# Mixer inputs taken from unscaled x and scaled out of PSUM, gate operands fetched from DRAM, LRU factor by exp, MLP operands at mixed spacing

## The chip, the cores and the metric

The kernel runs on one core of one Trainium2 chip. Its engines are TensorE (PE; its weight loads are listed as PEld), VectorE (DVE), ScalarE (ACT), GpSimd (POOL) and SyncE (SP, which issues DMAs here). The metric is device time in microseconds; lower is better.

## The reference

One decoder layer on 16 meta tokens and 512 tokens (T = 528) of width 2048, in float32:

```python
u = rmsnorm(h, norm1_g)
v_pool, v_lru, v_gelu, g_pool, g_lru = jnp.split(u @ w_in, ...)      # five times 2048
pool_out = pool_mixer(v_pool, pool_w, pool_scale)                    # window means, 512x512 maps
xc = causal_depthwise_conv(v_lru, conv_w, conv_b)                    # width 4
lru_out = rg_lru(xc, ...) * gelu(v_gelu)                             # h_t = a_t h_(t-1) + bt
merged = sigmoid(g_pool) * pool_out + sigmoid(g_lru) * lru_out
h = h + merged @ w_out
h = h + jnp.square(relu(rmsnorm(h, norm2_g) @ mlp_w1)) @ mlp_w2      # inner width 8192
out = rmsnorm(h, final_g)[:, 16:]
```

In `rg_lru`, r and i are sigmoids of 256x256 maps of each head of xc, a = exp(-8·r·softplus(-lam)) and bt = sqrt(1 - a²)·i·xc.

## The kernel before

Features lie on the 128 partitions, tokens on the free axis. Every float32 product is made of three matmuls: weights and inputs are split into a hi and a lo part (hi in the short fp32r format, lo = value - hi), and `mm3s` and `mm3` (matmul lines L332, L337) add hi·hi, hi·lo and lo·hi in PSUM. The class `Weights` runs through all weight chunks in one fixed order: SP loads a raw chunk (L94), VectorE forms sums for Strassen where wanted (L109, tile `sum`, or in place in `w21`), ACT writes `whi` (L117), VectorE `wlo` (L118). It works two chunks ahead of TensorE.

Each engine takes its instructions in the order in which the code was written, unless the framework puts one further on for priority. The stages, by time in the trace:

- Start and mixer, 0 to 515 us. A string of `jobs` sets the order: V2, VR, VL and VP are in_proj jobs (V2 and VL for the LRU branch, VR and VP for the pool branch; 96 matmuls of 264 columns for each 128 features, V2 and VR make two), GA_h holds the LRU gates of head h, PW_g the pool maps of group g, F_k forms Strassen operands of the normalised x for the later gates. V2 and VL_2 multiply x·g1 before the norm's scale is known (`split_x`), and their results are multiplied with `scale` in VR. While they run, ACT and DVE or POOL sum the squares; in VL_2 at k = 8 `norm1` adds them over the partitions and forms `scale` (a reciprocal and a Newton step). In VR every k's input is then scaled and split again (`rescale_x`, L361 to L363), and all further jobs use that. x lies in tile `a1`, as two halves of TH = 264 tokens (8 meta and 256 tokens), hi and lo blocks of 264 elements.
- `conv` makes xc and its hi and lo parts (`xs`, L454, L455), GA runs 48 matmuls and then tanh, sqrt, a reciprocal 1/(1+t) (L485), and the scan. in_proj results leave PSUM by ACT (`evac`, L408).
- Gates, 515 to 984: the three gated parts of w_in for the 512 tokens, 24 Strassens of 7 products. Each product is 24 matmuls of 256 columns and has one operand: x11, x21, x22 (quarters of x), t1 to t4 (their sums). x11, x21 and x22 are read straight from the blocks of 264 in `a1`, t2, t3 and t4 are brought from DRAM (`fill`, by POOL's queue), t1 stays in `a2`.
- w_out to 1176; first MLP matrix (w1), 1176 to 1788, 32 Strassens of the same kind with operands x11 ... t4 in blocks of 256; second MLP matrix (w2), 1788 to 2425, in 38 steps of 7 products over a window of eight slots in `a1`, `a2` and `slot0`, which hold t2, t4, t3, t1, x21, x22, x11 of one hidden block each (hi half, then lo half) and are split as they arrive; then the final norm to 2478.

A1's free space is counted in PL = 16·264 elements; HS is 256, `place(i)` names seven places for an operand.

## Time and profile before

| what | us |
|---|---|
| median of three runs | 2481.21 (2481.19 to 2487.64) |
| profiled execution | 2479.7 |
| its span in the trace | 2477.9 |
| TensorE busy | 2401.4 (97%) |
| VectorE busy | 1983.6 (80%) |
| ACT busy | 1196.9 (48%) |
| POOL busy | 288.5 (12%) |
| DMA moved | 407.71 MB, 165 GB/s mean |

The span runs from the first to the last instruction in the trace. Busy shares are means over stages that differ; what an engine does in one stage is read from that stage's window. "a" in a row is tile a1 or a2, "gs" a gate's sigmoid, "rx" rescaled x, "ga", "ps_vl", "ps_vp", "ps_vr" PSUM tiles of the jobs with those names.

### The profile page before, as it was taken

How to read it: one execution, taken by the hardware profiler on the slowest of the kernel's cores; microseconds unless marked ns; L12 is line 12 of the kernel's file. 1: busy time of each engine (PE TensorE's matmuls, PEld its weight loads, DVE VectorE, ACT ScalarE, POOL GpSimd, SP SyncE). 2: the span in 40 equal slices, each digit the busy share in tenths (PEclk: the TensorE clock that was granted, in tenths of full speed). 3: DMA queues.
4: the chain of work that ended last, by engine and by line, in shares of the span. 5: the costliest groups of instructions: out<-in, count | busy, mean ns of one | idle time of the engine just before them, and what ended most of it. 6: DMA issues, size and time to landing. Idle time of an engine off the chain costs nothing. (4 is left out here: it accounts for less than half of the span.)

```text
span 2477.9 us, 46247 instructions
## 1 busy us (share of the span) xinstructions
PE 2401.4 (97%) x19286; PEld 2345.5 (95%) x19286; DVE 1983.6 (80%) x2371; ACT 1196.9 (48%) x1639; POOL 288.5 (12%) x377
## 2 busy tenths in 40 slices
PE   7899999999999999999899999999989999999997
PEld 7899999989999999887899999999989999999996
DVE  8867676678888887368898889888788888888778
ACT  6444434345555555244444444444455555555445
POOL 2123232220000001022000000000100000000010
PEclk9999999999999999999999999999989999999999
DMA  5244443354444446567545444544565666665553
GB/s 208 77 141 137 158 136 137 127 187 139 147 143 145 139 143 246 193 203 256 192 159 168 155 156 161 168 153 156 211 174 158 189 179 184 181 179 174 150 167 106
DMA packets 114065, 407.71 MB, mean 165 GB/s; under 512 B 13440, under 2 KB 20736, under 8 KB 112448
## 3 DMA queue, kind: packets, MB, share of 16 engines
q1 hardware_dynamic: 78224, 251.82, 31.5%
q0 software_dynamic: 35488, 152.85, 19.1%
q8 instruction: 150, 2.46, 0.4%
q14 instruction: 59, 0.48, 0.1%
q10 hardware_dynamic: 144, 0.10, 0.0%
HBM read 319.91 MB, written 84.80 MB: 163 GB/s over the span
## 5 line engine op out<-in xcount | busy, mean ns | idle before, releaser
L118 DVE TENSOR_TENSOR wlo<-raw,whi 128x1024 fp32r<-128x1024 f32 (+6 forms) x403 | 468.1, 1164 | 167.3 <-ACT whi L117 164.1
L117 ACT ACTIVATE whi<-raw 128x1024 fp32r<-128x1024 f32 (+6 forms) x403 | 402.8, 1002 | 412.3 <-issue 105.1
L117 ACT ACTIVATE whi<-sum 128x1024 fp32r<-128x1024 f32 (+5 forms) x282 | 282.0, 1000 | 471.4 <-DVE sum L109 226.8
L118 DVE TENSOR_TENSOR wlo<-sum,whi 128x1024 fp32r<-128x1024 f32 (+5 forms) x282 | 322.5, 1144 | 89.7 <-ACT whi L117 85.6
L337 PE MATMUL ps_A<-a,whi 128*128 128x256 f32 x2048 | 357.4, 278 | 4.0 <-ACT p L600 1.7
L337 PE MATMUL ps_Ab<-a,whi 128*128 128x256 f32 x1728 | 315.4, 282 | 1.4 <-ACT u_b L622 0.7
L337 PEld LDWEIGHTS ps_A<-a,whi 128*128 128x128 f32 x2048 | 310.9, 189 | 5.9 <-ACT p L600 1.9
L337 PE MATMUL ps_A<-a,wlo 128*128 128x256 f32 x1024 | 283.9, 277 | 0.6 <-DVE wlo L118 0.6
L337 PEld LDWEIGHTS ps_Ab<-a,whi 128*128 128x128 f32 x1728 | 265.3, 189 | 2.5 <-ACT u_b L622 1.1
L337 PE MATMUL ps_Ab<-a,wlo 128*128 128x256 f32 x864 | 243.2, 282 | 0.0
L109 DVE TENSOR_TENSOR sum<-sum,raw 128x1024 f32<-128x1024 f32 (+7 forms) x188 | 215.2, 1145 | 5.6
L337 PEld LDWEIGHTS ps_A<-a,wlo 128*128 128x128 f32 x1024 | 193.3, 189 | 0.9 <-DVE wlo L118 0.8
L337 PE MATMUL ps_B<-a,whi 128*128 128x256 f32 x1024 | 178.6, 277 | 1.9 <-DMA a<-gsp_x 1.9
L337 PEld LDWEIGHTS ps_Ab<-a,wlo 128*128 128x128 f32 x864 | 166.2, 192 | 0.1
L337 PE MATMUL ps_Bb<-a,whi 128*128 128x256 f32 x864 | 158.3, 282 | 0.0
L337 PE MATMUL ps_wo<-a,whi 128*128 128x512 f32 x512 | 158.0, 390 | 0.0
L337 PEld LDWEIGHTS ps_B<-a,whi 128*128 128x128 f32 x1024 | 154.9, 189 | 2.1 <-ACT u L622 2.1
L332 PE MATMUL ps_vp<-a,whi 128*128 128x264 f32 x896 | 146.2, 285 | 7.5 <-ACT gs L471 4.8
L332 PE MATMUL ps_vl<-a,whi 128*128 128x264 f32 x896 | 146.1, 285 | 0.7 <-ACT gs L471 0.6
L337 PE MATMUL ps_B<-a,wlo 128*128 128x256 f32 x512 | 141.9, 277 | 0.3 <-DVE wlo L118 0.3
L337 PEld LDWEIGHTS ps_Bb<-a,whi 128*128 128x128 f32 x864 | 132.8, 189 | 0.0
L332 PEld LDWEIGHTS ps_vp<-a,whi 128*128 128x128 f32 x896 | 124.3, 188 | 8.4 <-ACT gs L471 5.5
(319 smaller groups left out, 5748.3 us busy)
## 6 DMA issues: line engine op xcount, KB each, us to landing
raw<-w SPq DMA_DIRECT2D x168, 512.0 KB, 4.2
raw<-w_in SPq DMA_DIRECT2D x135, 512.0 KB, 3.5
w<-w SPq DMA_DIRECT2D x56, 512.0 KB, 4.3
a<-ysp POOLq DMA_DIRECT2D x27, 896.0 KB, 6.4
hsp<-e POOLq DMA_DIRECT2D x32, 512.0 KB, 6.8
ysp<-t POOLq DMA_DIRECT2D x31, 512.0 KB, 4.4
w<-w_in SPq DMA_DIRECT2D x24, 512.0 KB, 3.5
ysp<-y POOLq DMA_DIRECT2D x31, 384.0 KB, 5.0
```

The source lines that it names most:

```text
L109: nc.vector.tensor_tensor(self.raw[o], self.raw[x], self.raw[y], op=ALU.add)
L117: nc.scalar.activation(hi[:, s], raw[:, s], AF.Copy)
L118: nc.vector.tensor_tensor(lo[:, s], raw[:, s], hi[:, s].bitcast(F32), op=ALU.subtract)
L332: PE.matmul(o, a, r, start=first and i == 0, stop=last and i == 2)
L337: PE.matmul(o, a, b, start=first and i == 0, stop=last and i == 2, skip_group_check=True)
```

## The change

The mixer's in_proj jobs all multiply the split of unscaled x·g1. `rescale_x` is gone; `norm1` runs in VR at k = 4. V2 and VL_2 leave PSUM by ACT as before and are multiplied with `scale` later; all other jobs leave PSUM by a multiplication with `scale` on VectorE. The first step of conv goes from VectorE to ACT. In `a1` the 528 tokens of a part follow each other, parts start every 576 elements (16 more for k of 8 and over). VL_3 comes before GA_0. The `xs` tiles lie in the pool of the Strassen sums, whose `w21` chunks can be loaded only after GA_7. In GA the reciprocal is replaced by exp(-2·...) on ACT, an addition of 1, and two scalar-tensor-tensor steps on VectorE (a Newton step from that start). F writes six operands to DRAM instead of three, and the gates' x11, t2, x21, t3 and x22 are fetched after VP_15, t4 after GA_7 and PW_3. In the gates x22 alone now has blocks every 264 elements, in w1 t4 alone, where all were at 256. In w2 the slots start every 3648 elements in `a1` (3584 before), a slot holds the values (then lo) first and hi after, and x11's hi part is moved by 0, 8, ..., 40 elements in six of nine slots; a slot is split in two pieces.

```diff
+SW = 2 * T
+XW = 576
...
-        self.free = {"raw": raw_bufs, "w21": 2}
+        self.free = {"raw": raw_bufs, "w21": 0}
...
-    def place(i):
+    def place(i, width=HS):
+        if width > HS:
+            return [tuple(a1[:, i * PL + (8 * j + k) * width : i * PL + (8 * j + k) * width + HS]
+                          for j in range(2)) for k in range(8)]
...
-    def fill(i, src, n):
-        if i < 6:
+    def fill(i, src, n, width=HS):
+        if width > HS:
+            t = a1[:, i * PL : i * PL + 16 * width].rearrange("p (a k n) -> p a k n", a=2, k=8)
+            src = src.rearrange("p a (k n) -> p a k n", k=8)
+            for j in range(2):
+                G.dma_start(t[:, j, :n, :HS], src[:, j, :n].bitcast(F32R))
+        elif i < 6:
...
     def ux(k, part):
...
-        a, kk = k // 8, k % 8
-        t = a1[:, 2 * a * PL : 2 * (a + 1) * PL].rearrange("p (b n) -> p b n", b=2)
-        at = part * 8 * TH + kk * TH
-        return t[:, :, at : at + TH]
+        at = (2 * k + part) * XW + 16 * (k // 8)
+        return a1[:, at : at + T]
...
-    jobs = "V2_0 VL_2 VR_0 GA_0 VL_3 VP_2 GA_1 VP_3 VL_4 PW_0 VL_5 F_0 VP_4 GA_2 VP_5 F_1 VL_6 VP_6 F_2 VL_7"
+    jobs = "V2_0 VL_2 VR_0 VL_3 GA_0 VP_2 GA_1 VP_3 VL_4 PW_0 VL_5 F_0 VP_4 GA_2 VP_5 F_1 VL_6 VP_6 F_2 VL_7"
...
+        V.tensor_scalar(sp8, sp4, -2.0, None, op0=ALU.mult)
...
-    f_sp = {r: dram.tile([P, 2, 8 * HS], F32, name=f"fsp_{r}") for r in ("t2", "t3", "t4")}
+    f_sp = {r: dram.tile([P, 2, 8 * HS], F32, name=f"fsp_{r}") for r in ("x11", "t2", "x21", "t3", "x22", "t4")}
...
         def split_x(k):
-            S.activation(ux(k, 0), blocks(ht[:, k]), AF.Copy, scale=pv("g1", k))
-            V.scalar_tensor_tensor(ux(k, 1), blocks(ht[:, k]), pv("g1", k),
-                                   ux(k, 0).bitcast(F32), op0=ALU.mult, op1=ALU.subtract)
-        def rescale_x(k):
-            x = tmp(f"rx{k}")[:, :T]
-            V.scalar_tensor_tensor(x, ht[:, k], pv("g1", k), scale, op0=ALU.mult, op1=ALU.mult)
-            S.activation(ux(k, 0), blocks(x), AF.Copy)
-            V.tensor_tensor(ux(k, 1), blocks(x), ux(k, 0).bitcast(F32), op=ALU.subtract)
...
+            S.activation(ux(k, 0), ht[:, k], AF.Copy, scale=pv("g1", k))
+            V.scalar_tensor_tensor(ux(k, 1), ht[:, k], pv("g1", k), ux(k, 0).bitcast(F32),
+                                   op0=ALU.mult, op1=ALU.subtract)
...
         def square_x(k):
...
-                (V, G)[k % 2].tensor_tensor(ssq[k % 2], ssq[k % 2], s, op=ALU.add)
+                V.tensor_tensor(ssq[k % 2], ssq[k % 2], s, op=ALU.add)
...
+        PARTS = ((slice(0, MH), slice(0, META)), (slice(MH, TH), slice(META, T)))
         def evac(t, out):
...
-            for s, o in ((slice(0, MH), out[:, :META]), (slice(MH, TH), out[:, META:])):
-                S.activation(blocks(o), t[:, :, s], AF.Copy)
-        xc, pend = {}, []
+            for s, o in PARTS:
+                V.tensor_tensor(blocks(out[:, o]), t[:, :, s], blocks(scale)[:, :, s], op=ALU.mult)
+        def raw(t, out):
+            for s, o in PARTS:
+                S.activation(blocks(out[:, o]), t[:, :, s], AF.Copy)
+        def scaled(v):
+            for s, o in PARTS:
+                V.tensor_tensor(blocks(v[:, o]), blocks(v[:, o]), blocks(scale)[:, :, s], op=ALU.mult)
+        xc, xs, pend = {}, {}, []
+        def early(c, t):
+            v = keep(f"v{c}")
+            V.memset(v[:, :3], 0.0)
+            raw(t, v[:, 3:])
+            pend.append((c, v))
...
         def job_V2(c):
...
-            pend.extend((c + j, evac_v(c + j, ts[j])) for j in range(2))
+            for j in range(2):
+                early(c + j, ts[j])
...
         def job_VR(c):
...
-            ts = in_proj("ps_vr", 2, rescale_x)
+            ts = in_proj("ps_vr", 2, lambda k: norm1() if k == 4 else None)
...
+                scaled(v[:, 3:])
...
         def job_VL(c):
+            t, = in_proj(f"ps_vl{c}_", 1)
...
-                t, = in_proj("ps_vl2_", 1, lambda k: norm1() if k == 8 else None)
-                pend.append((c, evac_v(c, t)))
+                early(c, t)
...
-                t, = in_proj(f"ps_vl{c}_", 1)
-                conv(c, evac_v(c, t))
+                v = tmp(f"v{c}")
+                V.memset(v[:, :3], 0.0)
+                evac(t, v[:, 3:])
+                conv(c, v)
...
         def conv(c, v):
...
-            V.tensor_scalar(x, v[:, 3:], pv("cw3", c), pv("cb", c), op0=ALU.mult, op1=ALU.add)
+            S.activation(x, v[:, 3 : 3 + T], AF.Identity, scale=pv("cw3", c), bias=pv("cb", c))
...
-            hi, lo = (xs_at(2 * (c % 3) + i) for i in range(2))
+            t = sums_pool.tile([P, SW], F32R, tag=("sum", "w21")[c % 2], name=f"xs{c}", bufs=2)
+            hi, lo = xs[c] = t[:, :T], t[:, T:]
...
-                        xh, xl = (xs_at(2 * ((2 * hd + ci) % 3) + i) for i in range(2))
+                        xh, xl = xs[2 * hd + ci]
...
-            rec = {}
+            e1 = {}
...
-                r = pt[0, co]
-                S.activation(r, r, AF.Tanh, scale=sp4[:, 2 * hd + co : 2 * hd + co + 1])
-                y = rec[co] = tmp(f"y{hd}{co}")[:, :T]
-                V.tensor_scalar(y, r, 1.0, None, op0=ALU.add)
+                c, r = 2 * hd + co, pt[0, co]
+                e = e1[co] = tmp(f"e{hd}{co}")[:, :T]
+                S.activation(e, r, AF.Exp, scale=sp8[:, c : c + 1])
+                S.activation(r, r, AF.Tanh, scale=sp4[:, c : c + 1])
+                S.activation(e, e, AF.Copy, bias=1.0)
...
-                S.activation(pt[0, co], pt[0, co], AF.Sqrt)
-            for co in range(2):
-                V.reciprocal(rec[co], rec[co])
+                r, e = pt[0, co], e1[co]
+                n = tmp(f"n{hd}{co}")[:, :T]
+                V.scalar_tensor_tensor(n, r, 1.0, e, op0=ALU.add, op1=ALU.mult)
+                V.scalar_tensor_tensor(n, n, -4.0, e, op0=ALU.add, op1=ALU.mult)
+                e1[co] = n
+                S.activation(r, r, AF.Sqrt)
...
-                m, i, y = pt[0, co], pt[1, co], rec[co]
-                V.scalar_tensor_tensor(m, m, 2.0, y, op0=ALU.mult, op1=ALU.mult)
+                m, i, n = pt[0, co], pt[1, co], e1[co]
+                V.scalar_tensor_tensor(m, m, -0.5, n, op0=ALU.mult, op1=ALU.mult)
...
-                V.tensor_scalar(y, y, 2.0, -1.0, op0=ALU.mult, op1=ALU.add)
+                V.tensor_scalar(n, n, -0.5, -1.0, op0=ALU.mult, op1=ALU.add)
...
-                V.tensor_tensor_scan(x, y, i, 0.0, op0=ALU.mult, op1=ALU.add)
+                V.tensor_tensor_scan(x, n, i, 0.0, op0=ALU.mult, op1=ALU.add)
...
         def job_F(k):
...
+            put_hl(t1, *place(4)[k])
+            for r, x in (("x11", x11), ("t2", t2), ("x21", x21)):
+                spill(tmp(f"f{r}{k}")[:, :SEQ], x, f_sp[r], k)
...
-            put_hl(t1, *place(4)[k])
-            for r, x in (("t2", t2), ("t3", t3), ("t4", t4)):
+            for r, x in (("t3", t3), ("x22", x22), ("t4", t4)):
...
             if (kind, i) == ("VP", 15):
-                fill(1, f_sp["t2"], 8)
-            elif kind == "GA" and i == 7:
-                fill(6, f_sp["t4"], 8)
-        fill(5, f_sp["t3"], 8)
+                for q, r in ((0, "x11"), (1, "t2"), (2, "x21"), (6, "t3")):
+                    fill(q, f_sp[r], 8)
+                fill(3, f_sp["x22"], 8, TH)
+            elif (kind, i) == ("GA", 7):
+                W.free["w21"] = 2
+        fill(5, f_sp["t4"], 8)
...
-    X = {r: place(i) for r, i in (("t2", 1), ("t1", 4), ("t3", 5), ("t4", 6))}
-    for r, i in (("x11", 0), ("x21", 2), ("x22", 3)):
-        X[r] = [tuple(a1[:, i * PL + (8 * j + k) * TH + MH : i * PL + (8 * j + k + 1) * TH] for j in range(2))
-                for k in range(8)]
+    X = {r: place(i, TH if r == "x22" else HS) for r, i in (
+        ("x11", 0), ("t2", 1), ("x21", 2), ("x22", 3), ("t1", 4), ("t4", 5), ("t3", 6))}
...
-    X = {r: place(i) for r, i in (("t2", 0), ("t3", 1), ("x22", 2), ("t4", 3), ("x11", 4), ("t1", 5), ("x21", 6))}
+    X = {r: place(i, TH if r == "t4" else HS) for r, i in (
+        ("t2", 0), ("t3", 1), ("x22", 2), ("t4", 3), ("x11", 4), ("t1", 5), ("x21", 6))}
...
-        fill(q, g_sp[("t2", "t3", "x22", "t4")[q]], 7)
+        fill(q, g_sp[("t2", "t3", "x22", "t4")[q]], 7, TH if q == 3 else HS)
...
-    places = {i: a[:, q * n : (q + 1) * n]
-              for a, held in ((a1, (1, 2, 3, 7, 8)), (a2, (4, 5, 6))) for q, i in enumerate(held)}
+    gaps = {i: 8 * q for q, i in enumerate((1, 2, 3, 7, 8, 0))}
+    places = {i: a[:, q * step : q * step + n + gaps.get(i, 0)]
+              for a, held, step in ((a1, (1, 2, 3, 7, 8), n + 64), (a2, (4, 5, 6), n)) for q, i in enumerate(held)}
...
     def load_slot(j, queue):
...
-            slots[j] = places[j % (WIN + 1)].rearrange("p (a n) -> p a n", a=2)
-            queue.dma_start(slots[j][:, 1].bitcast(F32), y_sp[j])
+            s = slots[j] = places[j % (WIN + 1)]
+            queue.dma_start(s[:, : 7 * HS].bitcast(F32), y_sp[j])
+    def slot(j, r):
+        s, a = slots[j], slice(0, 6 * HS) if r is None else at(r)
+        h = 13 * HS + gaps.get(j % (WIN + 1), 0) if r == "x11" else 7 * HS + a.start
+        return s[:, h : h + a.stop - a.start], s[:, a]
...
     def split_slot(j):
...
-            hi, lo = slots[j][:, 0], slots[j][:, 1]
-            S.activation(hi, lo.bitcast(F32), AF.Copy)
-            V.tensor_tensor(lo, lo.bitcast(F32), hi.bitcast(F32), op=ALU.subtract)
+            for r in (None, "x11"):
+                hi, lo = slot(j, r)
+                S.activation(hi, lo.bitcast(F32), AF.Copy)
+                V.tensor_tensor(lo, lo.bitcast(F32), hi.bitcast(F32), op=ALU.subtract)
...
+            places[0] = s0.tile([P, 14 * HS + 40], F32R, name="slot0")
...
-        strassen(f"b{t}", lambda r: [tuple(slots[j][:, i, at(r)] for i in range(2)) for j in js], put_plain(e),
+        strassen(f"b{t}", lambda r: [slot(j, r) for j in js], put_plain(e),
```

On VectorE at the start, before: from the first step on the summed squares on. `ssq` holds them, `n1a` and `n1b` are work tiles, `rx` is rescaled x, `a_84` is a1, `wlo` a weight's lo part.

```order
L310 TENSOR_SCALAR n1a<-ssq_196 128x528
L312 RECIPROCAL scale<-n1b 128x528
L118 TENSOR_TENSOR wlo_781<-raw_460,whi_780 128x1024
L313 TENSOR_TENSOR n1b<-scale 128x528
L314 TENSOR_TENSOR n1b<-n1b,n1a 128x528
L315 TENSOR_SCALAR n1b<-n1b 128x528
L316 TENSOR_TENSOR scale<-scale,n1b 128x528
L361 SCALAR_TENSOR_TENSOR rx_646<-ht,par,scale 128x528
L361 SCALAR_TENSOR_TENSOR rx_662<-ht,par,scale 128x528
L361 SCALAR_TENSOR_TENSOR rx_678<-ht,par,scale 128x528
L363 TENSOR_TENSOR a_84<-rx_646,a_84 128x2x264
```

And after, the same place; `v` are the LRU inputs, `xc` the conv's results:

```order
L315 TENSOR_SCALAR ssq_204<-ssq_202 128x528
L317 RECIPROCAL scale<-ssq_205 128x528
L120 TENSOR_TENSOR wlo_857<-raw_575,whi_856 128x1024
L318 TENSOR_TENSOR ssq_205<-scale 128x528
L120 TENSOR_TENSOR wlo_863<-raw_629,whi_862 128x1024
L319 TENSOR_TENSOR ssq_205<-ssq_205,ssq_204 128x528
L320 TENSOR_SCALAR ssq_205<-ssq_205 128x528
L321 TENSOR_TENSOR scale<-scale,ssq_205 128x528
L418 TENSOR_TENSOR v_514<-v_514,scale 128x16
L418 TENSOR_TENSOR v_514<-v_514,scale 128x512
L418 TENSOR_TENSOR v_518<-v_518,scale 128x16
L418 TENSOR_TENSOR v_518<-v_518,scale 128x512
```

Scale is now followed by the six multiplications of the early jobs' results and their conv, where the products of x with scale and the splits had stood; two weight splits stand between its steps instead of one.

On POOL around VP_15, before; `pw` are the window sums of the pool branch, `gs` gate values, `fsp` the operands in DRAM, `pl` what the pool branch spills:

```order
L509 TENSOR_TENSOR pw14_8_4929<-pw14_4_4927 128x513
L204 DMA a1_84<-fsp_t2_180 128x4096
L509 TENSOR_TENSOR pw15_1_5289<-pv15_5286 128x527
L509 TENSOR_TENSOR pw15_2_5291<-pw15_1_5289 128x525
L509 TENSOR_TENSOR pw15_4_5293<-pw15_2_5291 128x521
L509 TENSOR_TENSOR pw15_8_5295<-pw15_4_5293 128x513
L208 DMA a2_930<-fsp_t4_182 128x2560
L490 TENSOR_TENSOR gs710_5345<-gs710_5345,xc14_5048 128x528
L490 TENSOR_TENSOR gs711_5360<-gs711_5360,xc15_5170 128x528
L207 DMA a1_84<-fsp_t4_182 128x1536
```

And after:

```order
L526 TENSOR_TENSOR pw14_8_5025<-pw14_4_5023 128x513
L215 DMA a1_84<-fsp_x11_180 128x4096
L215 DMA a1_84<-fsp_t2_181 128x4096
L526 TENSOR_TENSOR pw15_1_5381<-pv15_5378 128x527
L215 DMA a1_84<-fsp_x21_182 128x4096
L526 TENSOR_TENSOR pw15_2_5383<-pw15_1_5381 128x525
L218 DMA a1_84<-fsp_t3_183 128x1536
L526 TENSOR_TENSOR pw15_4_5385<-pw15_2_5383 128x521
L211 DMA a1_84<-fsp_x22_184 128x8x256
L526 TENSOR_TENSOR pw15_8_5387<-pw15_4_5385 128x513
L211 DMA a1_84<-fsp_x22_184 128x8x256
L507 TENSOR_TENSOR gs710_5443<-gs710_5443,xc14_5144 128x528
```

Five operands' fetches (t3 in part) now stand between the sums of channels 14 and 15, where one stood; x22 takes two DMAs.

## Rows read from the trace of the kernel before

**Rows 1.** The page's first section: span; busy time, share of span and instructions by engine.

```profile
span 2477.9 us, 46247 instructions
...
PE 2401.4 (97%) x19286; PEld 2345.5 (95%) x19286; DVE 1983.6 (80%) x2371; ACT 1196.9 (48%) x1639; POOL 288.5 (12%) x377
```

**Rows 2.** Windows: length; busy (count) of PE, PEld, DVE, ACT, POOL; granted clock; DMA share; GB/s.

```profile
47.00:108.80 61.80, 47.29 (x336) 45.74 (x337) 57.30 (x75) 29.25 (x45) 5.65 (x4) 0.86 0.14 48
109.00:515.00 406.00, 395.04 (x3025) 383.75 (x3024) 279.30 (x343) 172.44 (x264) 122.21 (x124) 1.00 0.42 141
1878.00:2392.80 514.80, 514.80 (x4373) 514.80 (x4372) 412.37 (x394) 256.07 (x316) 38.64 (x56) 1.00 0.62 177
```

**Rows 3.** TensorE's waits up to 109 us: for whom; total us, times, longest us.

```profile
PE ps_vr L332 <- ACT a L362: 7.3, 1, 7.3
...
PE ga L332 <- ACT a L454: 4.6, 2, 3.6
```

**Rows 4.** VectorE's timeline at the scale: start, us, line, operation, tiles, shape, count.

```profile
45.66 3.45 DVE L312 RECIPROCAL scale<-n1b 128x528 f32<-128x528 f32 x1 [0.71 <-ACT n1b L311]
...
52.79 2.13 DVE L361 SCALAR_TENSOR_TENSOR rx<-ht,par,scale 128x528 f32<-128x528 f32 x3
```

**Rows 5.** Windows after two waits of the start, columns as in rows 2.

```profile
50.00:60.00 10.00, 5.66 (x24) 5.35 (x25) 9.86 (x17) 3.87 (x6) 0.00 (x0) 0.52 0.16 52
84.00:91.00 7.00, 4.70 (x18) 4.08 (x18) 6.98 (x10) 1.97 (x4) 0.81 (x1) 0.53 0.35 128
```

**Rows 6.** Windows: two gate products, Strassens of gates and w1, job VL, job GA.

```profile
712.31:715.15 2.84, 2.84 (x27) 2.84 (x25) 2.81 (x3) 2.39 (x3) 0.00 (x0) 1.00 0.30 115
715.15:717.87 2.72, 2.72 (x27) 2.72 (x25) 2.72 (x4) 1.35 (x3) 0.00 (x0) 1.00 0.54 190
712.31:731.71 19.40, 19.40 (x171) 19.40 (x169) 15.42 (x16) 9.59 (x12) 0.00 (x0) 1.00 0.32 107
1369.76:1388.80 19.04, 19.04 (x171) 19.04 (x169) 17.01 (x22) 9.21 (x11) 1.08 (x2) 1.00 0.48 159
457.52:469.29 11.77, 11.77 (x98) 11.77 (x97) 5.41 (x8) 3.73 (x6) 5.14 (x4) 1.00 0.31 106
120.59:126.41 5.82, 5.82 (x51) 5.82 (x49) 3.23 (x4) 5.42 (x9) 1.54 (x1) 1.00 0.57 203
```

**Rows 7.** Chain that ended last, 1860 to 1910: start, us, engine, tile, matmuls.

```profile
1868.52 2.38 PE ps_Ab L337 x21
...
1883.35 2.83 PE ps_Bb L337 x24
```

**Rows 8.** Timelines: weight loads at 1877.7, then the matmul at 2394.39 with its wait.

```profile
1877.65 0.19 PEld L337 LDWEIGHTS ps_Bb<-a,wlo 128*128 128x128 f32 x1
1877.78 0.30 PEld L337 LDWEIGHTS ps_Ab<-slot,whi 128*128 128x128 f32 x2
...
2394.39 0.39 PE L337 MATMUL ps_Cb<-a,wlo 128*128 128x256 f32 x1 [1.30 <-DVE wlo L118]
```

**Rows 9.** Lines: instructions, ns min/median/max, first and last start us, shapes.

```profile
L485 DVE RECIPROCAL y<-y x16: 3444/3450/3454, 100.2 to 508.3; 128x528 f32<-128x528 f32 x16
...
L361 DVE SCALAR_TENSOR_TENSOR rx<-ht,par,scale x16: 759/764/769, 52.8 to 72.8; 128x528 f32<-128x528 f32 x16
...
L408 ACT ACTIVATE v<-ps_vl x28: 155/374/592, 47.8 to 482.1; 128x16 f32<-128x16 f32 x14, 128x512 f32<-128x512 f32 x14
...
L483 ACT ACTIVATE gs<-gs x16: 642/646/647, 100.6 to 507.8; 128x528 f32<-128x528 f32 x16
...
L483 ACT ACT_TABLE_LOAD  x8: 1283/1283/1283, 99.3 to 504.1; - x8
...
L654 DVE SCALAR_TENSOR_TENSOR e<-ps_Ab,q_b x38: 415/418/426, 1794.8 to 2428.2; 128x256 f32<-128x256 f32 x38
```

**Rows 10.** DMA, 485 to 530 in 40 slices; a fill: issues, KB each, us to landing.

```profile
GB/s 15 226 226 248 277 408 408 390 368 226 15 7 0 0 164 309 419 264 9 208 371 331 186 69 0 15 219 15 233 291 393 408 364 233 390 408 386 328 397 408
...
a<-fsp_t POOLq DMA_DIRECT2D x2, 2048.0 KB, 9.7
```

More of the change, by code (lines that the diff above doesn't have):

```diff
@@ L91, in _load @@
         pool, bufs = (self.pool, self.raw_bufs) if tag == "raw" else (self.sums, 2)
-        t = pool.tile([P, CH], F32, tag=tag, name=f"{tag}{i}", bufs=bufs)[:, :n]
+        t = pool.tile([P, CH if tag == "raw" else SW], F32, tag=tag, name=f"{tag}{i}", bufs=bufs)[:, :n]
         for s in self._cuts(i, n):
@@ L106, in _split @@
             if o not in self.raw:
-                t = self.sums.tile([P, CH], F32, tag="sum", name=f"sum{o[1]}", bufs=2)
+                t = self.sums.tile([P, SW], F32, tag="sum", name=f"sum{o[1]}", bufs=2)
                 self.raw[o] = t[:, : self.raw[x].shape[-1]]
@@ L172, in build @@
     spt = [const.tile([P, KD], F32, name=f"spt{i}") for i in range(5)]
+    sp8 = spt[1]
     scale = const.tile([P, T], F32, name="scale")
@@ L354, in split_x @@
         def split_x(k):
-            S.activation(ux(k, 0), blocks(ht[:, k]), AF.Copy, scale=pv("g1", k))
-            V.scalar_tensor_tensor(ux(k, 1), blocks(ht[:, k]), pv("g1", k),
-                                   ux(k, 0).bitcast(F32), op0=ALU.mult, op1=ALU.subtract)
-        def rescale_x(k):
-            x = tmp(f"rx{k}")[:, :T]
-            V.scalar_tensor_tensor(x, ht[:, k], pv("g1", k), scale, op0=ALU.mult, op1=ALU.mult)
-            S.activation(ux(k, 0), blocks(x), AF.Copy)
-            V.tensor_tensor(ux(k, 1), blocks(x), ux(k, 0).bitcast(F32), op=ALU.subtract)
-        ssq = [keep(f"ssq{i}")[:, :T] for i in range(2)]
+            S.activation(ux(k, 0), ht[:, k], AF.Copy, scale=pv("g1", k))
+            V.scalar_tensor_tensor(ux(k, 1), ht[:, k], pv("g1", k), ux(k, 0).bitcast(F32),
+                                   op0=ALU.mult, op1=ALU.subtract)
+        nx = x_stage.enter_context(tc.tile_pool(name="nx", bufs=1))
+        ssq = [nx.tile([P, T], F32, name=f"ssq{i}") for i in range(4)]
         def square_x(k):
@@ L372, in square_x @@
                 S.activation(s, ht[:, k], AF.Square)
-                (V, G)[k % 2].tensor_tensor(ssq[k % 2], ssq[k % 2], s, op=ALU.add)
+                V.tensor_tensor(ssq[k % 2], ssq[k % 2], s, op=ALU.add)
         def norm1():
-            a, b = tmp("n1a"), tmp("n1b")
             for h in range(2):
@@ L381, in norm1 @@
                 V.tensor_copy(ssq[0][:, s], t[:, :TH])
-            rms_scale(scale, ssq[0], a[:, :T], b[:, :T])
+            rms_scale(scale, ssq[0], ssq[2], ssq[3])
         def psum_v(name):
@@ L389, in products @@
             s = slice(k % 8 * P, (k % 8 + 1) * P)
-            mh, ml = ([ux(k, i)[:, b] for b in range(2)] for i in range(2))
+            mh, ml = ([ux(k, i)[:, b * TH : (b + 1) * TH] for b in range(2)] for i in range(2))
             for (hi, lo), t in zip(ws, ts):
@@ L425, in job_VR @@
             for i, v in pend:
-                for at, s in ((3, slice(0, MH)), (3 + META, slice(MH, TH))):
-                    o = blocks(v[:, at : at + 2 * (s.stop - s.start)])
-                    V.tensor_tensor(o, o, blocks(scale)[:, :, s], op=ALU.mult)
+                scaled(v[:, 3:])
                 conv(i, v)
@@ L859, in at, with shift @@
         return slice(i * HS, (i + n) * HS)
-    def shift(pool, name):
-        V.memset(pool.tile([P, 8], F32, name=name), 0.0)
+    def shift(pool, name, n=8):
+        V.memset(pool.tile([P, n], F32, name=name), 0.0)
     slots, early, n = {}, late.enter_context(ExitStack()), 14 * HS
-    places = {i: a[:, q * n : (q + 1) * n]
-              for a, held in ((a1, (1, 2, 3, 7, 8)), (a2, (4, 5, 6))) for q, i in enumerate(held)}
+    gaps = {i: 8 * q for q, i in enumerate((1, 2, 3, 7, 8, 0))}
+    places = {i: a[:, q * step : q * step + n + gaps.get(i, 0)]
+              for a, held, step in ((a1, (1, 2, 3, 7, 8), n + 64), (a2, (4, 5, 6), n)) for q, i in enumerate(held)}
     def load_slot(j, queue):
         if j < JS:
-            slots[j] = places[j % (WIN + 1)].rearrange("p (a n) -> p a n", a=2)
-            queue.dma_start(slots[j][:, 1].bitcast(F32), y_sp[j])
+            s = slots[j] = places[j % (WIN + 1)]
[4 more added lines that the diff above has]
+        return s[:, h : h + a.stop - a.start], s[:, a]
     def split_slot(j):
         if j < JS:
-            hi, lo = slots[j][:, 0], slots[j][:, 1]
-            S.activation(hi, lo.bitcast(F32), AF.Copy)
-            V.tensor_tensor(lo, lo.bitcast(F32), hi.bitcast(F32), op=ALU.subtract)
+            for r in (None, "x11"):
+                hi, lo = slot(j, r)
+                S.activation(hi, lo.bitcast(F32), AF.Copy)
+                V.tensor_tensor(lo, lo.bitcast(F32), hi.bitcast(F32), op=ALU.subtract)
     for j in range(32):
@@ L886, in build @@
             s0 = early.enter_context(tc.tile_pool(name="s0", bufs=1, side="right", reuse_waits="tile"))
-            places[0] = s0.tile([P, 14 * HS], F32R, name="slot0")
-            shift(s0, "shift0")
+            places[0] = s0.tile([P, 14 * HS + 40], F32R, name="slot0")
+            shift(s0, "shift0", 32)
         def of(r, n=1):
```

8 lines of the change are left out of this document (removed).

## The prediction

> **What bounds the kernel now.** I read the page's first section, then the program by stage (busy time per engine), then TensorE's waits, then single products of each stage by windows cut at their ends, and last the rows around the two places where TensorE's pace changes. The first section says that TensorE is busy in 2401.4 of 2477.9 us [rows 1]; in the stretch from 1878 to 2392.8, inside the last weight matrix, it is busy throughout, while VectorE is busy in 412 of 515 us [rows 2]. So a gain can come only from two things: the 76.5 us in which TensorE does nothing, or the length of one matmul.
>
> The idle time has one large place. From 47.0 (VL_2's last matmul) to 108.8 (VL_3's last) 61.80 us pass, TensorE is busy in 47.29, at a mean granted clock of 0.86 [rows 2]. It waits 7.3 us for the first rescaled x (L362) and 4.6 us for xs's hi half (L454) [rows 3]. VectorE shows why VR waits: the reciprocal of the scale starts at 45.66 and takes 3.45 us, four more steps follow, and the first product with scale (L361) starts at 52.79 [rows 4]. After that wait the clock is 0.52 from 50 to 60 us, and 0.53 from 84 to 91 [rows 5], the lower of its two levels, 1.2 of 2.4 GHz, each time just after TensorE had stood.
>
> The length of a matmul is not one number. In one Strassen of the gates, the product that ends at 715.15 takes 2.84 us and the next 2.72, both for 24 matmuls of 256 columns (the counts in the rows take in three that overlap an end) [rows 6]. The first reads x11 through blocks that start every 264 elements (1056 bytes), the other t1, whose blocks follow every 256. In w1 all operands lie at 256: a Strassen takes 19.04 us, seven times 2.72; a gate Strassen, with three operands at 264, takes 19.40 = 4×2.72 + 3×2.84 [rows 6]. And there is a second, lasting pace: up to 1878 the second weight matrix runs at 2.38 us for 21 matmuls, 113.3 ns, and from 1883 on at 2.83 us for 24, 117.9 ns, with no wait at the turn [rows 7]. It starts where a run of weight loads is a little late: the row of 1877.65 is followed by one at 1877.78, 0.13 us on instead of 0.11, and it ends after a wait of 1.30 us before 2394.39 [rows 8]. The granted clock is 1.00 throughout [rows 2].
>
> **The change part by part.** The sum is made against the profiled execution, 2479.7 us (span 2477.9 and 1.8 around it); the median of the runs is 1.5 us above that, which I leave out.
>
> 1. Start. VR no longer waits for scale: it multiplies the unscaled split, which is in place since V2, and only its evacuation needs scale. The sixteen rescalings go (DVE 2×16, ACT 16). The sum of squares' matmuls move from VL_2 into VR, so they cost TensorE the same. VL_3 runs before GA_0. What the stretch of 61.80 us needs at the full clock is VR's 192 matmuls and VL_3's 96 at 11.77/96 = 122.6 ns and GA_0's 48 at 5.82/48 = 121.2 ns [rows 6]: 23.5 + 11.8 + 5.8 = 41.1 us. So 20.7 us can go. What would be late next is scale itself for VL_3's and VR's evacuations, and xs for GA_0: its sums are formed after the fifth of VR's sixteen k, 7.4 us into it, near 54; from the reciprocal's start to L361 7.1 us pass [rows 4] and about two lie before it (an estimate), so 63; six multiplies, and conv and splits for v0 and v1, take some 10 us more (an estimate from forms of 0.4 to 0.8 us), 73; GA_0 starts at 47 + 23.5 + 11.8 = 82. Nine us of cover; I take −20, bounds −20.7 and −10 (half lost to a PSUM bank that waits for scale).
>
> 2. Gates. x11 and x21 move to blocks of 256 elements, x22 stays at 264. Two products in each of 24 Strassens go from 2.84 to 2.72: 48 × 0.12 = −5.8, bounds −5.8 and 0.
>
> 3. Second weight matrix. x11's hi parts are now shifted against the others by 0 to 40 elements. In the gates a product at other spacing is followed by products of 2.72 [rows 6], so I take it that one such product per step brings the short pace back. The 4373 matmuls from 1878 to 2392.8 take 514.80 us [rows 2], 117.7 ns each; at 113.3 they take 19.2 less. Against it stand the shifted products: 26 steps, one each, 0.12 × 6/9 (six of nine places are shifted) = +2.1. Sum −17.1, bounds −19.2 and +2.1 (the long pace stays). Its cover is VectorE, busy 412 of 515 us; the change splits each slot in two pieces, 30 more small instructions on VectorE and on ACT in some 500 us, which the idle fifth takes.
>
> 4. First weight matrix. t4 goes from 256 to 264: 32 × 0.12 = +3.8, bounds 0 and +3.8.
>
> 5. Mixer's pace. The two halves of a 264-column operand now follow each other directly, as they do in xs before. That gate product takes 121.2 ns, the in_proj 122.6 [rows 6]: 32 jobs of 96 matmuls, 3072 × 1.4 = −4.3, I take −4. The bounds are −17 (the short pace of rows 7 for 264 columns, 113.3 × 264/256 = 116.8, over 3072 matmuls) and +4 (the same step the other way).
>
> 6. Engines in the mixer. DVE loses 16 reciprocals of 3450 ns (55 us), 16 rescale products of 764 ns and their subtractions [rows 9]; it gains 32 scalar-tensor-tensors, which by that same form cost at most 0.76 each (24 us), 30 evacuations of 16 and 512 columns, which from 418 ns for 256 columns out of PSUM come to 0.8 to 0.9 each (an estimate, 26 us), and smaller ones: about −26 us of 279. ACT gives up 30 evacuations of 155 + 592 ns (22 us) and sixteen splits, and gains 32 passes of 646 ns, eight table loads of 1283 ns [rows 9], the convs' first step and three more spills per F job: about +20 on 172 [rows 2]. Both stay below 0.75 busy in a stretch where TensorE is busy 395 of 406. ACT's chain behind a gate's last sigmoid grows by 3.9 us (two exps and two adds of 0.65 and a table load); queued behind it is the next whi split, for which TensorE waits once its two chunks ahead, 11.8 us of matmuls, are used up. I take 0, bounds −6 (a wait of GA goes, DVE being freer) and +8 (one us per head, eight heads).
>
> The Trainium skill (ScalarE: Activation LUTs, What ACT_TABLE_LOAD costs) gives about 1283 ns for the load and 1380 ns for a drain beside it, which for eight more switches would make +21 instead of +10 us on ACT; no row here shows the drain as idle time, and even so ACT would stay below half busy.
>
> 7. Fills. Four operands and the first part of t3, 4.4 × 2048 KB = 9.2 MB, are fetched from VP_15 on, where before one operand and part of another were. They are needed from about 515 on, one every 2.8 us, so x22 near 526; t4, issued after GA_7, is the last, near 532. Before, the queue moved up to 408 GB/s around 491 to 495, and one fill landed in 9.7 us [rows 10]. From some 487 on, at 390 GB/s, the 9.2 MB take 24 us: 511, in time. One after the other at 9.7 they would take 42: 529, three too late, and the gates' weight loads that share the DMA engines could bring as much again. On POOL the fills stand between the pool branch's sums, so that a fill held for its place also holds PW_3. I take 0, the nearer to the rate that was reached; bounds −2 (PW_3's own wait shrinks) and +8.
>
> Sum: −20 −5.8 −17.1 +3.8 −4 +0 +0 = −43; 2479.7 − 43 = 2437. Its own range is 2424 to 2452.
>
> **The rivals.** A, the above. B: the long pace of the second matrix stays, since nothing shows that a shift inside one operand, and by 8 elements only, does what a spacing of 264 does in the gates; for it speaks that some shifts are small, against it that eight slots with different shifts are mixed in a product. Then term 3 is +2.1: 2456.
> C: place does not matter to a matmul, and 2.84 and 2.72 differ for some other reason, such as the order of products. Then terms 2 to 5 are nothing: 2480 − 20 = 2460. Against it: three products of seven in one Strassen, each time those at 264, are the long ones [rows 6].
> The Trainium skill has a rule for it (TensorE: Matmul & The Clock Gate, Step-by-step: what each phase is for): the streaming operand and the weight load have read ports of their own, and loading the next weights takes no read bandwidth from the running matmul. By that rule an operand's address could not matter; the 2.84 beside the 2.72 speaks against it here.
> D: the mixer too comes down to the short pace, term 5 at −17: 2424.
> E: the start gives half, because VR's banks are held until scale is there and GA_0 waits: 2447.
> F: the change doesn't do what it says: VR's and VL_3's evacuations wait for scale as long as the products did, term 1 is 0: 2457.
> G, slower: an operand at another phase is what puts TensorE into the long pace, and the products after it keep it, since w1 and w2 have no wait to end it. Gates: 24 × (6×2.83 + 2.84 − 19.40) = +10.1; w1: 32 × (6×2.83 + 2.84 − 19.04) = +25.0; w2 +2.1; start −20, mixer −4: +13, 2493. It decides if more than about six tenths of the equal-spaced products run at the long pace. For it: w1, with none of them, is at the short pace now [rows 6]; against it: in the gates the short ones directly follow the long ones.
>
> **How the numbers follow.** A 57%, B 14%, C 6%, D 8%, E 6%, F 3%, G 6%. The likeliest is A: 2437. A range that holds eight in ten must take in D, E, B and C, and leaves out G and the ends: 2418 to 2462. A measurement of this kernel can tell 0.3%, 7.4 us, from no change: all but G and the end of C and F lie below 2473.8, so faster 0.91, same 0.04, slower 0.05.
>
> **What would show it.** Term 1: no wait of VR's first matmuls after VL_2, a granted clock of 1.0 from 47 on, and GA_0 without a wait; the time from VL_2's end to GA_0's and VL_3's near 41 us. Terms 2 and 4: windows of single products, 2.72 for x11 and x21 in the gates, 2.84 for t4 in w1; a Strassen of 19.16 in both. Term 3: 113.3 ns in the chain of waits over the whole second matrix. Term 5: a VL or VP job in 11.6 us. Term 6: no wait for whi of over a microsecond per head. Term 7: no wait for a DMA at the first seven products of the gates. It is wrong if a long pace stands in the gates or in w1, or if TensorE waits behind the new exps or fills for more than 10 us in all.

## The result and the profile after

The changed kernel took 2451.99 us (median of three, 2448.87 to 2453.86) against 2481.21: 0.9894 of the kernel before, interval 0.9848 to 0.9939. That is 29 us less, where 43 were forecast; it lies in the stated range. Set side by side by where TensorE's first matmul of each stage stands in the two traces (the last matrix, w2, reaches from 1788.6 to 2429.7 before, and not to 2425 as the text on the kernel says):

| stretch | before | after | difference | forecast |
|---|---|---|---|---|
| to VP_2's first matmul | 108.8 | 90.0 | -18.8 | -20 |
| rest of the mixer | 406.1 | 407.1 | +1.0 | -4 |
| gates | 469.3 | 461.1 | -8.2 | -5.8 |
| w_out | 175.0 | 175.0 | 0 | 0 |
| w1 with its seam | 629.5 | 639.4 | +9.9 | +3.8 |
| w2 | 641.0 | 628.6 | -12.4 | -17.1 |
| rest | 48.2 | 48.6 | +0.4 | 0 |

Three stretches are off by more than 4 us: w2 gave less, and the end of the mixer and the seam at the start of w1 cost what had been put at nothing. The table sets one execution against one. In the profiles further below, whose code in the stretch is the same, the rest of the mixer took 408.8 to 411.7 us, w1 with its seam 635.8 to 640.5 and w2 625.9 to 630.1. The page's first section, as in [rows 1]:

```profile
span 2449.8 us, 46429 instructions
...
PE 2383.4 (97%) x19286; PEld 2327.9 (95%) x19286; DVE 1939.2 (79%) x2444; ACT 1222.4 (50%) x1676; POOL 298.1 (12%) x399
```

TensorE's waits of the changed kernel up to 109 us, as in [rows 3]; VR waits for nothing any more, and GA_0 for little:

```profile
PE ps_v L337 <- ACT whi L119: 6.6, 1, 6.6
PE ga L337 <- ACT gs L483: 1.1, 1, 1.1
PE ga L337 <- DVE pv L409: 0.4, 1, 0.4
PE ga L337 <- DVE v L409: 0.3, 1, 0.3
```

Windows of the changed kernel, columns as in [rows 2]: VR to GA_0 (answers to the first of [rows 2]), the ten microseconds of [rows 5], the rest of the mixer, a gate Strassen, one of w1, a VL job (these as in [rows 6]):

```profile
45.76:90.00 44.24, 42.79 (x347) 42.13 (x346) 33.87 (x48) 19.46 (x25) 2.89 (x2) 1.00 0.24 79
50.00:60.00 10.00, 10.00 (x79) 9.74 (x78) 5.29 (x5) 2.27 (x3) 0.00 (x0) 1.00 0.08 30
90.00:497.08 407.08, 390.05 (x3026) 378.78 (x3025) 265.75 (x409) 209.15 (x294) 146.94 (x153) 0.99 0.51 173
555.63:574.79 19.16, 19.16 (x170) 19.16 (x169) 17.28 (x18) 10.53 (x13) 2.14 (x4) 1.00 0.59 216
1370.19:1389.35 19.16, 19.16 (x171) 19.16 (x170) 17.00 (x22) 9.20 (x11) 1.08 (x2) 1.00 0.47 162
446.81:458.39 11.58, 11.58 (x99) 11.58 (x97) 7.15 (x9) 3.49 (x4) 0.00 (x0) 1.00 0.42 137
```

The granted clock is at 1.00 where it had been 0.52, a Strassen takes the forecast 19.16 us in gates and w1, a VL job 11.58 instead of 11.77. In the rest of the mixer TensorE is busy 5.0 us less than in [rows 2], and idle 6.1 us more: the gain of the pace is there, and is lost to a wait. TensorE's timeline names it, and ACT's says what it waited for:

```profile
490.09 1.22 PE L337 MATMUL ps_pw<-a,whi 128*128 128x512 f32 x2 [8.53 <-ACT po L548]
```

```profile
482.00 1.28 ACT L493 ACT_TABLE_LOAD   x1
483.29 1.36 ACT L493 ACTIVATE e<-gs,spt 128x528 f32<-128x528 f32 x2
484.56 0.72 ACT L494 ACTIVATE gs<-gs,sp 128x528 f32<-128x528 f32 x1
485.19 0.63 ACT L495 ACTIVATE e<-e 128x528 f32<-128x528 f32 x1
485.72 0.72 ACT L494 ACTIVATE gs<-gs,sp 128x528 f32<-128x528 f32 x1
486.35 0.63 ACT L495 ACTIVATE e<-e 128x528 f32<-128x528 f32 x1
486.99 1.28 ACT L502 ACT_TABLE_LOAD   x1
488.28 1.18 ACT L502 ACTIVATE gs<-gs 128x528 f32<-128x528 f32 x2
489.37 0.67 ACT L548 ACTIVATE po<-ps_pw,par 128x512 f32<-128x512 f32 x1
```

PW_3 has two PSUM banks. Both are full when GA_7's last sigmoid ends, and their eviction (L548) is queued on ACT behind GA_7's whole chain, 7.4 us of it. Before, the longest such wait was 2.2 us. The wait also costs clock, as the window right after it shows:

```profile
490.00:495.00 5.00, 4.91 (x16) 3.92 (x17) 3.58 (x5) 1.65 (x3) 1.19 (x2) 0.70 0.61 190
```

In the same window the granted clock is 0.50 to 0.63 in profiles of the next section with the same mixer and the same wait. There TensorE is busy 391.7 to 393.7 us in the rest of the mixer, not 390.05, so the profile shown here is the mildest case.

The chain of waits of the changed kernel in w2, as in [rows 7]; ps_Ab x48 is a step's last product and the next step's first, x11:

```profile
1919.63 5.52 PE ps_Ab L342 x48
1925.15 2.72 PE ps_Bb L342 x24
...
1938.75 5.51 PE ps_Ab L342 x48
1944.26 2.83 PE ps_Bb L342 x24
...
1955.57 2.83 PE ps_Bb L342 x24
1958.39 5.67 PE ps_Ab L342 x48
1964.06 2.74 PE ps_Bb L342 x24
```

After some x11 products the pace is short, after others the whole step stays long, until the next x11. Of 24 steps with eight slots 15 take 19.1 to 19.2 us and nine 19.7 to 19.8, and the long ones repeat with a period of nine steps, the number of slots. Of the three long steps in each nine, two follow a short step, as the one at 1938.75 does: there the shifted x11 product stands between a short pace and a long one. All nine profiles with these shifts have the same nine long steps. All 24 took 19.8 before.

### The profile page after: what moved, and what is told of

Read it like the earlier page. It is cut to its first block, busy times and chain, and to the rows that moved or that the text cites. A ratio compares the mean times of both kernels' runs of the same rounds, so it can differ in the third digit from the quotient of the medians.

```text
span 2449.8 us, 46429 instructions
## 1 busy us (share of the span) xinstructions
PE 2383.4 (97%) x19286; PEld 2327.9 (95%) x19286; DVE 1939.2 (79%) x2444; ACT 1222.4 (50%) x1676; POOL 298.1 (12%) x399
## 5 line engine op out<-in xcount | busy, mean ns | idle before, releaser
L342 PE MATMUL ps_A<-a,whi 128*128 128x256 f32 x2048 | 363.0, 280 | 5.0 <-ACT p L621 2.0
L111 DVE TENSOR_TENSOR sum<-w,raw 128x1024 f32<-128x1024 f32 (+7 forms) x94 | 107.3, 1141 | 44.2 <-DMA raw<-w 39.5
```

Source lines behind the costliest of these rows:

```text
L111: nc.vector.tensor_tensor(self.raw[o], self.raw[x], self.raw[y], op=ALU.add)
L342: PE.matmul(o, a, b, start=first and i == 0, stop=last and i == 2, skip_group_check=True)
```

## The experiments

All but the last are the changed kernel with one edit. The times of a kernel spread by up to 1% here, for a reason that the third and fourth run show, so that stage lengths of the profiles decide, beside the medians. The changed kernel's 2451.99 us stems from another set of runs than the experiments; the kernel before had medians from 2481.2 to 2486.0 us in these sets, so a difference of a few us to 2452 alone shows nothing.

**PW's eviction on VectorE.**

```diff
-                S.activation(z, t, AF.Copy, scale=pv("ps", c))
+                V.tensor_scalar(z, t, pv("ps", c), None, op0=ALU.mult)
```

> The changed kernel with one line moved: the pool maps' results leave PSUM by VectorE (tensor_scalar) instead of ACT. Theory: TensorE's 8.5 us wait in PW_3 is ACT's queue, in which the exps, tanhs, additions, roots and table loads of GA_7 stand ahead of the eviction; with the eviction on VectorE the wait falls under 3 us and the mixer ends about 6 us sooner: 2446 against 2452, ratio to the kernel before 0.986. Rival: what holds PW_3 is the fills, which stand between POOL's window sums of channel 15: the wait stays near 8 us and the time at 2452.

2451.55 us (2444.21 to 2457.42; ratio 0.9895, interval 0.985 to 0.994). The wait in PW_3 went only from 8.5 to 7.1 us, now for VectorE, and waits of PW in other groups made up for it (9.8 us in all, where it was 9.6). The wait is for the eviction on either engine, not for the fills; but moving the eviction alone did not help, since on VectorE it stands behind the Newton steps, which wait for the same exps.

**The reciprocal again.** L485's reciprocal, the addition of 1 on VectorE and the factors 2 and -1 of before, in place of exp and the Newton steps.

> The changed kernel with the LRU's reciprocal back on VectorE in place of exp, addition and the Newton steps. Theory: exp costs ACT 3.9 us per head and buys nothing, since VectorE had room; without it the wait in PW_3 falls from 8.5 us to the 2 to 3 of before and the time by about 5 us, to 2447. Rival: VectorE is what the mixer is short of, so that 16 reciprocals of 3.45 us show again in waits for xs or for evacuations on VectorE: 2455 or more.

2458.8 us (2455.19 to 2461.76; ratio 0.9931, interval 0.9903 to 0.996): 7 us slower than the changed kernel, with intervals that overlap. The wait in PW_3 fell to 4.8 us, part of what the theory had, but another came, as the trace's waits between 84 and 520 us say:

```profile
PE ps_Agl L342 <- ACT p_gl L617: 5.5, 1, 5.5
PE ps_pw L337 <- ACT po L544: 4.8, 1, 4.8
```

The gates took 470.4 us instead of 461.1, and the mixer's rest 409.2, no less than with exp, since waits of 1.8 us for whi, 0.6 for wlo and 0.6 more for an evacuation came up in it. ACT's timeline says what the first eviction of the gates (p_gl) waited for, and POOL's what stood ahead of that; then the landing of the LRU's stores (issues, KB each, median us), here and in the changed kernel:

```profile
511.43 0.38 ACT L617 ACTIVATE p_gl<-ps_Agl 128x256 f32<-128x256 f32 x1 [4.43 <-DMA lr<-xc]
```

```profile
498.00 0.56 POOL L215 DMA_DIRECT2D a<-fsp_t  x1
498.53 0.56 POOL L508 DMA_DIRECT2D lr<-xc  x1
```

```profile
lr<-xc POOLq DMA_DIRECT2D x2, 256.0 KB, 11.9
```

```profile
lr<-xc POOLq DMA_DIRECT2D x2, 256.0 KB, 2.4
```

With PW_3 done sooner, the fill of t4 goes out ahead of the LRU's stores, and these land after 12 us; in the changed kernel they go out first (497.55 and 500.18, the fill at 501.24). So this version lost its time at the gates to an order of transfers, not to VectorE. The theory's 2447 fell, and the rival's time came, but not by the waits that it named; what exp with Newton steps is worth by itself is not shown.

**No shift in w2.**

```diff
-    gaps = {i: 8 * q for q, i in enumerate((1, 2, 3, 7, 8, 0))}
+    gaps = {}
```

> The changed kernel without the shifts of x11's hi parts in the second matrix (slot starts as changed). Theory: the shifts are what brings the short pace back, so without them one late weight load leaves the matmuls at 117.8 ns: second matrix near the 641 us of before instead of 628.6, 2464. Rival 1: the slots' new starts did it: 2452 or, without the shifted products, 2450. Rival 2: it is chance when the long pace begins, and here it doesn't: 2443.

2445.81 us in the median, but in two groups: 2439.61, 2440.51, 2445.22, 2446.39 and 2458.65, 2462.14. The profiled one is the last: w2 took 640.2 us, all 24 full steps 19.8. So the slots' new starts do not bring the short pace back (rival 1); between the theory and rival 2 the next run decides.

**The same kernel once more.**

> The changed kernel without the shifts in the second matrix, word for word the kernel of the earlier look, whose profiled execution took 2462 us while four of its other five took 2440 to 2446. Theory: the pace is a matter of chance from execution to execution, so that the same code shows the second matrix either near 640 us (long pace) or near 621 (short pace all through, short of the shifted products too): 2462 or 2441. Rival: the two groups of times come from elsewhere (waits, the seam before the first matrix), and the second matrix takes 640 us again whatever the total.

2443.83 us in one execution, and w2 took 617.3, all 24 full steps 19.0 to 19.1. The chains of the two executions of the same code, a few products after 1904, first the one of 2462 us, then this one:

```profile
1904.27 2.83 PE ps_Bb L342 x24
1907.09 2.83 PE ps_Ab L342 x24
```

```profile
1904.34 2.72 PE ps_Bb L342 x24
1907.06 2.72 PE ps_Ab L342 x24
```

So without shifts the long pace is a matter of chance from execution to execution: 640.2 or 617.3 us with one program. It would explain the kernel before too: of 42 executions of it beside these experiments 11 took 2460 to 2472 us, 29 took 2479 to 2493 and two 2504 to 2506, groups about 20 us apart, which is the forecast's 19.2 us for a w2 at the long pace. The profile of before is one with the long pace; that the lower group is one without it is inferred, as no profile of it was taken. Against that group, whose median is 2464.0 us, the change gains 12 us and not 29.

The same profile shows the long pace in w1, and what ended it. Its fourth and fifth Strassen:

```profile
1218.87:1238.68 19.81, 19.81 (x171) 19.81 (x169) 17.58 (x22) 9.33 (x12) 1.08 (x2) 1.00 0.51 168
1238.68:1257.84 19.16, 19.16 (x171) 19.16 (x169) 16.93 (x22) 9.21 (x11) 1.08 (x2) 1.00 0.47 158
```

The fourth runs at the long pace to its end, although a product with t4 at 264 stands just ahead of it; after its own t4 the pace is short to the end of the stage.

**Shifts that grow evenly.**

```diff
-    gaps = {i: 8 * q for q, i in enumerate((1, 2, 3, 7, 8, 0))}
+    gaps = {i: 8 * max(0, (i - 4) % 9 - 1) for i in range(9)}
...
-            a2 = pool.tile([P, 42 * HS], F32R, name="a2")
+            a2 = pool.tile([P, 42 * HS + 8], F32R, name="a2")
```

> The changed kernel with x11's hi parts shifted by 0, 0, 8, 16, ... 56 elements over slots 4, 5, 6, 7, 8, 0, 1, 2, 3, so that neighbouring slots of a step differ by 8 elements but for one pair, where the change has three neighbours without a shift. Theory: the return to the short pace comes of a shift that grows from matmul to matmul, as with operands at 264; then the nine of 24 full steps that now take 19.8 us come down to 19.15: -6, 2446. Rival: which slots end the x11 product decides, whatever the shifts: as many long steps as now, 2450 to 2454.

2446.14 us (2443.07 to 2451.31; ratio 0.988, interval 0.9836 to 0.9923). Two long steps of 24 are left of nine, nine steps apart; the 24 full steps sum to 461.3 us against 465.0 of the change, 474.9 at the long pace and 457.0 at the short one. All of w2 took 625.0 instead of 628.6. The theory holds in part and gave 3.7 us of the 6, because two long steps stay and its own shifted products are a little longer (a short step is 19.2 instead of 19.1).

**t4 of w1 in blocks of 256** (without the width TH in place and fill).

> The changed kernel with t4 of the first MLP matrix back in blocks of 256 elements, so that no product there has other spacing. Theory: the spaced product is an insurance that costs 0.12 us per Strassen: 19.04 instead of 19.16 us, 3.5 us less, as long as no late weight load starts the long pace (as in the kernel before); where one does, the long pace stays to the end of the stage: up to 30 x 0.74 = 22 us more, so profiles and times fall into two groups. Rival: the pace of this stage does not hang on t4: 2452 in every run, Strassens of 19.16.

2446.92 us (2441.19, 2446.88, 2446.97 and one of 2467.7; ratio 0.9878, interval 0.9814 to 0.9942). A Strassen of its profile:

```profile
1370.22:1389.26 19.04, 19.04 (x171) 19.04 (x169) 17.00 (x22) 9.21 (x11) 1.08 (x2) 1.00 0.49 160
```

From the fourth Strassen on w1 took 552.2 us instead of 555.6: 3.4 us, the price of the spaced product. The 2467.7 is 21 us above the others, as expected where the long pace begins and nothing ends it, but it was not profiled.

**x22 of the gates in blocks of 256.**

> The changed kernel with x22 of the gates in blocks of 256 elements too. Theory: 24 x 0.12 = 2.9 us less where the short pace holds (gates 458 instead of 461), up to 24 x 0.76 = 18 us more where the long pace begins early and nothing ends it. Rival: the operand's spacing does not matter: 461 as now.

2448.36 us (2447.62 to 2453.17; ratio 0.9875, interval 0.9823 to 0.9927); the gates took 458.4 us, at the short pace from the second Strassen on:

```profile
556.17:575.21 19.04, 19.04 (x171) 19.04 (x169) 17.29 (x18) 10.52 (x13) 2.14 (x4) 1.00 0.64 218
```

**PW_3 ahead of GA_7.**

```diff
-    jobs += " VL_13 VP_12 GA_6 VP_13 VP_14 VL_14 VL_15 VP_15 GA_7 PW_3"
+    jobs += " VL_13 VP_12 GA_6 VP_13 VP_14 VL_14 VP_15 VL_15 PW_3 GA_7"
```

> The changed kernel with the last jobs in the order VP_15, VL_15, PW_3, GA_7 (fills after VL_15), so that PW_3's evictions stand ahead of GA_7's exps and roots on ACT and VectorE. Theory: the 8.5 us wait in PW_3 goes and the mixer ends some 6 us sooner: 2446. Rival: GA_7's chain then stands ahead of the gates' first splits and evictions, and the wait moves there (the first gate Strassen 4 to 6 us longer): 2450 to 2454.

2465.03 us (2458.79 to 2470.04; ratio 0.993, interval 0.9905 to 0.9956). The rival won, and by more than it said: TensorE waits for nothing in PW_3, but 5.3 us in GA_7 for its first sigmoids and 12.6 for the gates' first eviction, and the gates take 477.6 us. Waits between 84 and 560 us, then that eviction on ACT:

```profile
PE ps_Agl L342 <- ACT p_gl L621: 12.6, 1, 12.6
PE ga L337 <- ACT gs L483: 6.4, 2, 5.3
```

```profile
516.88 0.38 ACT L621 ACTIVATE p_gl<-ps_Agl 128x256 f32<-128x256 f32 x1 [7.20 <-DMA lr<-xc]
```

It waits for the store of the LRU's last result, which lands at 516.78, 2.3 us after its issue: the end of GA_7's chain, now inside the gates, holds their first eviction.

**The mixer's layout as before**, `ux` and what reads it, all else as changed.

> The changed kernel with x in the mixer laid out as before (two blocks of 264 per part, parts 264 apart, the second half of the tokens elsewhere), all else as changed. Theory: the layout sets the in_proj matmuls' pace: back from 120.4 to 122.3 ns, 3072 x 1.9 = 5.8 us more in start and mixer (VR's and VL_3's 288 matmuls 0.5 us of it). Rival: the pace comes of the lighter engines beside it, not of addresses: 120.4 stays.

2453.34 us in one execution. VL and VP matmuls take 122.3 ns again in the mean, instead of 120.4; a VP job's window:

```profile
450.71:462.47 11.76, 11.76 (x99) 11.76 (x97) 6.15 (x8) 3.54 (x4) 0.00 (x0) 1.00 0.42 135
```

The rest of the mixer took 413.7 us against 407.1 to 412.1 in the others with its queue order unchanged. The layout sets this pace; the engines' load has no part in it that shows.

**GA_0 ahead of VL_3.**

> The changed kernel with GA_0 ahead of VL_3 again, as before. Theory: the order is a good part of the start's gain, because after VR the scale's multiplications, conv and the splits for GA_0 need some 10 us, which VL_3 covers: GA_0 now waits 6 to 10 us and the clock drops beside it, so that the stretch from VR's start to VP_2's grows from 44.2 to 52 or more. Rival: the unscaled inputs alone did it, and xs is ready in VR's shadow: 44 to 46.

2448.70 us in one execution. From VR to VP_2 47.9 us instead of 44.2, less than the theory's 8 us more and at a granted clock of 1.00, and the rest of the mixer took 406.4, so that the gates began at 498.1, no later than in other runs. The order is worth 4 us on the spot and nothing that shows at the mixer's end.

**More banks for PW.**

```diff
-                t = ps1.tile([P, 512], F32, tag="p1", name=f"ps_pw{c}")
+                    tp = psum_v(f"ps_pw{c}_")
+                t = tp[:, m % 2]
```

> The changed kernel with the pool maps' results in pairs in the in_proj jobs' PSUM tiles (three of them) instead of two single banks, so that TensorE can go through PW_3 while ACT is still at GA_7's exps and roots. Theory: the wait of 8.5 us is one for a bank; with banks enough PW_3 runs through, ACT catches up in part during its 5.6 us: mixer and first gate Strassen together 4 to 6 us less, 2447. Rival: ACT's queue is the bound whichever bank is free; the wait moves to the gates' first weight split or eviction, and the sum stays within 2 us.

2460.54 us (2460.03 to 2462.8; ratio 0.9918, interval 0.9876 to 0.996): wrong both ways. The pairs share the PSUM tiles of the in_proj jobs, and the mixer's rest grew to 421.9 us with waits such as these:

```profile
PE ps_pw__2982 L337 <- ACT po L549: 4.6, 1, 4.6
PE ps_pw__5486 L337 <- ACT gs L483: 4.0, 1, 4.0
PE ps_vl L337 <- ACT gs L483: 2.9, 2, 2.0
PE ps_pw__5486 L337 <- ACT po L549: 2.9, 1, 2.9
```

**Both together**, pairs of banks and even shifts.

> The pairs of banks for the pool maps and the evenly growing shifts of the second matrix together. Theory: the two add up: 6 us of the second matrix and 4 to 6 of the mixer's end, 2441, ratio to the kernel before 0.984. Rival: only the shifts count: 2446.

2456.39 us (2454.45 to 2458.54; ratio 0.9892, interval 0.9865 to 0.9919): the shifts' part again (two long steps), and the banks' loss. No version is shown to beat the changed kernel clearly; the medians of several, the even shifts among them, are 3 to 8 us lower, with intervals that overlap or from one execution.

## Why the prediction was right, and where a size was off

- Term 1, the start, was right: 18.8 of 20, no wait in VR, the clock at 1.00. What it gave as the cover of GA_0, VL_3 ahead of it, was worth 4 of them on the spot.
- Term 2 was right in its mechanism: 48 × 0.12 us, 19.40 to 19.16, and x22's own removal gave 2.7 more where it was tried. The other 2.6 us came in the first Strassen of the gates, 20.2 us instead of 22.8: before, TensorE waited there 1.5 us for splits of weights (whi, wlo) and 0.8 for an eviction, after, 0.4 for a split. Why these came sooner was not tried.
- Term 3 was mis-sized. "One such product per step brings the short pace back" holds for 15 of 24 steps, and for 22 with the even shifts. So the set of shifts decides; which property of it does is not shown: with the even shifts seven steps in nine hold the one pair of neighbours without a shift between them, and six of the seven are short. And the term was measured against an execution at the long pace, of which I did not know that it is chance: without shifts and at the short pace the full steps take 457.0 us, so the shifts then cost 8.0 us in them, and 11.3 in all of w2 (628.6 against 617.3). Of the three long steps in nine one is rival B, the long pace staying; the other two come after a short step, which is what rival G said of a product at another phase.
- Term 4 was right: 3.4 us, measured by undoing it. The rest of w1's +9.9 lies in its seam, the first three Strassens: 83.7 us against 77.3. Before, the clock held in the second half of it, after, it fell again, as it did in all twelve experiments (from 50 to 77 us into w1 it is 1.00 before and 0.81 to 0.94 in the thirteen). Windows of before, then of after:

```profile
1209.20:1219.20 10.00, 10.00 (x91) 10.00 (x89) 7.20 (x10) 1.95 (x2) 0.54 (x1) 1.00 0.67 226
1219.20:1231.20 12.00, 9.23 (x77) 8.63 (x76) 11.94 (x14) 7.46 (x11) 1.08 (x2) 1.00 0.46 165
```

```profile
1184.00:1194.00 10.00, 9.48 (x68) 9.49 (x69) 8.21 (x11) 0.49 (x1) 0.54 (x1) 0.83 0.61 205
1194.00:1206.00 12.00, 9.27 (x54) 8.58 (x53) 9.11 (x11) 6.19 (x9) 1.08 (x2) 0.73 0.45 169
```

  In the twelve experiments the seam took 80.1 to 84.6 us, with t4's fill in one piece too (82.6), so that fill is not the cause. Why the clock falls there and the seam is 3 to 7 us longer than in the one profile of before stays open.
- Term 5 was right: 1.9 ns instead of 1.4 per matmul, and by the layout alone. In the length of the stretch it does not show, as term 6 took it back.
- Term 6, put at 0, was the step that failed: 6.1 us more idle, and in other profiles up to 3.6 us more of matmuls at a lowered clock behind it. The price of the chain, 3.9 us more per head, was right, but its cover, two weight chunks, is that of an in_proj job. Behind GA_7 stands PW_3, which needs its banks evicted by the same queue. The cures tried only moved the wait: the eviction on VectorE and the other order to VectorE and into the gates, the pairs of banks to other groups. With the reciprocal PW_3 waits 3.7 us less, and the gates then wait for a store that a fill has overtaken, a collision that the term did not look at.
- Term 7 held: no DMA wait at the gates.
- Rival C is out: undoing the place alone moved 19.16 to 19.04 twice and 120.4 to 122.3 ns once. With it goes the prediction's reading of the rule of the Trainium skill (TensorE: Matmul & The Clock Gate, Step-by-step: what each phase is for), that an operand's address could not matter; the rule itself is about read ports and the weight load, and no run here tests that.
- Rival G did not come as a whole: in the profiles with a spaced product in each Strassen no long pace held to the end of gates or w1. But it stood there for whole Strassens in four of the experiments' profiles (19.7 to 19.8 us each; in the gates with the reciprocal and with PW_3 first, in w1 in the second run without shifts and in the last), and one or two spaced products passed before one ended it.
